# Four 32 KB places as pools in the order of the bytes, behind 72 instead of 64 loads of 8 KB

## The chip, the cores and the metric

The kernel runs on one core of one Trainium2 chip. The metric is the device time of one execution in microseconds. All work is in float32 (some operands of the first half are split into a rounded part and a rest), and all weights come from HBM by DMA.

## The reference, cut to what matters

One encoder layer over 512 tokens of width 1024: a mixer (projections, banded attention, a short convolution, gates), then a layer norm, then a mixture of 16 experts in which each expert picks its 64 best tokens, then a layer norm.

```python
logits = jnp.einsum('bsd,de->bse', x, w_router)
aff = jax.nn.softmax(logits, axis=-1)
top_val, top_idx = lax.top_k(jnp.swapaxes(aff, 1, 2), cap)
xe = x[b_idx, top_idx]
h = jax.nn.silu(jnp.einsum('becd,edf->becf', xe, w_gate)) * jnp.einsum('becd,edf->becf', xe, w_up)
ye = jnp.einsum('becf,efd->becd', h, w_down) * top_val[..., None]
return jnp.zeros_like(x).at[b_idx, top_idx].add(ye)
```

The change touches only how the experts' weights `w_gate`, `w_up` and `w_down` get into the core: 16 experts of 3 matrices of 1024 x 2048, 403 MB in all.

## The kernel before

The mixer runs first, to about 520 us of the span. Then a loop over 8 pairs of experts follows (`for p in range(NPAIR)`). The host lays the weights of a pair out as 12 groups `w_moe[p, g]` of [128 partitions, 4 units, 2048 numbers]. A unit is 8 KB in each of 128 partitions (1 MB in all), a group is 32 KB in each partition (4 MB). So a pair has 48 units: units 0 to 31 are gate and up in turn (four blocks `cb` of eight units, line 963), units 32 to 47 are down (four blocks `cq`, line 1009). A unit of either kind is multiplied once and is then of no more use. Beside these matmuls, TensorE gathers the tokens of the next pair (line 898), turns (lines 913, 984) and scatters the results (line 1022).

`fetch(p, m)` hands out unit m of pair p. Units are numbered through, `n = 48 * p + m`. The first 64 units (`SMALL`) are loads of their own, of 8 KB in a partition, called `w_n`. They go to the places that the list `places` names, in its order:

```python
places = slots[:7] + [(wk, "W2")] + slots[7:8] + [(wk, "W0")] + slots[8:]
places += [(extra, "E")] + slots + [(extra, "E")] + slots[2:] + [(extra, "E")]
```

`slots` are the 20 pools R0 to R19 of 8 KB each, which lie one behind another in a partition. Units 1 to 22 are loaded ahead; from unit 23 on each load takes the place of an older unit. Counted along the list, units 45 to 62 lie on R2 to R19 in this order and unit 63 lies on E. R0 and R1 become the accumulators of the output.

From unit 64 on (pair 1, group 4) the weights come in whole groups `w_p_g` of 32 KB in a partition, into four places of that size. Before, these are one pool with `bufs=4`, opened over the bytes of R4 to R19, which `small.close()` gives back. In the last pair, the groups from 4 on are filled by four loads each.

All these loads are issued by SyncE (SP) on one DMA queue, in the order of the program (`pin`). SP waits, at each load, until the units that lay on the place have been read, and everything behind it in SP's order waits too. `reuse_waits="tile"` makes such a wait one for the tiles that lay on the bytes in question.

Of the kernel before, what the change touches and what calls it, by code (L numbers as in the profile page):

```python
# [10 lines left out]
F32 = mybir.dt.float32  # L11
# [7 lines left out]
P = 128  # L19
# [20 lines left out]
def encoder_layer(ctx: ExitStack, tc: tile.TileContext, x, ln0r, ln0c, w_in, conv_w, sink, w_ao, w_co, w_out,  # L40
# [5 lines left out]
    extra = ctx.enter_context(tc.tile_pool(name="extra", bufs=1))  # L46
# [7 lines left out]
    def shaped(t, shape):  # L54
        names = "abcd"[:len(shape)]
        return t[:, :int(np.prod(shape))].rearrange(f"p ({' '.join(names)}) -> p {' '.join(names)}",
                                                    **dict(zip(names, shape)))
# [279 lines left out]
    src, nm, _ = loads[0]  # L337
# [244 lines left out]

    UNITS, SMALL = 48, 64
    units, groups = {}, {}

    def load_unit(n, pool, tag):
        t = pool.tile([P, 2048], F32, tag=tag, name=f"w_{n}")
        p, m = n // UNITS, n % UNITS  # L590
        pin(nc.sync.dma_start(t, w_moe[p, m // 4][:, m % 4]))
        return t

    def fetch(p, m):

        n = UNITS * p + m
        if n < SMALL:
            if n not in units:
                units[n] = load_unit(n, *places.pop(0))
            return units.pop(n)  # L600
        if not big:
            small.close()
            big.append(ctx.enter_context(tc.tile_pool(name="big", bufs=4, reuse_waits="tile")))
        g, j = m // 4, m % 4
        if j == 0:
            t = big[0].tile([P, 4, 2048], F32, tag="G", name=f"w_{p}_{g}")
            src = w_moe[p, g]
            if p < NPAIR - 1 or g < 4:
                pin(nc.sync.dma_start(t, src))
            for i in range(4 if p == NPAIR - 1 and g >= 4 else 0):  # L610
                if (g, i) != (UNITS // 4 - 1, 3):
                    pin(nc.sync.dma_start(t[:, i], src[:, i]))
                else:
                    ends, begin = shaped(t[:, i], [2, 4, 256]), shaped(src[:, i], [2, 4, 256])
                    for f, n in ((0, 2), (2, 1), (3, 1)):
                        pin(nc.sync.dma_start(ends[:, :, f:f + n, :], begin[:, :, f:f + n, :]))
            groups[p, g] = t
        return groups[p, g][:, j]
# [208 lines left out]
    t = NT - 1  # L827
# [44 lines left out]
    small = ExitStack()  # L872
    accp = ctx.enter_context(tc.tile_pool(name="accp", bufs=1, reuse_waits="tile"))
    slots = [(accp, "R0"), (accp, "R1")]
    for i in range(2, 20):
        slots.append(((ctx if i < 4 else small).enter_context(tc.tile_pool(name=f"r{i}", bufs=1, reuse_waits="tile")), f"R{i}"))
    places = slots[:7] + [(wk, "W2")] + slots[7:8] + [(wk, "W0")] + slots[8:]
    places += [(extra, "E")] + slots + [(extra, "E")] + slots[2:] + [(extra, "E")]
    big = []
    for n in range(1, 23):  # L880
        units[n] = load_unit(n, *places.pop(0))
# [68 lines left out]
    for p in range(NPAIR):  # L950
# [3 lines left out]
        for cb in range(NCB):  # L954
            pss = [mmt(f"p{nm}_{p}_{cb}") for nm in "gu"]
            for kq in range(4):
                for i in range(2):
                    wt = shaped(fetch(p, 8 * cb + 2 * kq + i), [2, 2, 512])
                    for k in range(2):
                        kk = 2 * kq + k  # L960
                        for a in range(2):
                            hs = slice(64 * a, 64 * a + 64)
                            pin(nc.tensor.matmul(pss[i][hs, :], xe[:, kk, hs], wt[:, a, k, :], start=(kk == 0), stop=(kk == KT - 1)))  # L963
                    for _ in range(2 * i if p == cb == 0 else 1 - i):
                        if pend:
                            pend.pop(0)()
# [34 lines left out]
        for cq in range(4):  # L1001
            pd = mmt(f"d_{p}_{cq}")
            for fq in range(4):
                wt = shaped(fetch(p, 32 + 4 * cq + fq), [2, 4, 256])
                for ft in range(4):
                    f = 4 * fq + ft
                    for a in range(2):
                        hs = slice(64 * a, 64 * a + 64)
                        pin(nc.tensor.matmul(pd[hs, :256], hTs[p][:, f, hs], wt[:, a, ft, :], start=(f == 0), stop=(f == 15)))  # L1009
                for _ in range(2):  # L1010
                    if pend:
                        pend.pop(0)()
# [33 lines left out]
    sd, v, r, a2, nb = (q2[:, i, :] for i in range(5))  # L1046
# [80 lines left out]
```

## Time and profile before

| | us |
|---|---|
| median of 3 runs | 1470.6 (1470.47 to 1473.98) |
| profiled execution, its own time | 1468.77 |
| its span, first to last instruction | 1467.0 |
| busy in the span: TensorE matmuls | 1374.0 (94%) |
| busy: VectorE, ScalarE, GpSimd | 396.8, 291.8, 61.8 |

The DMA queue of SP (q1) moves 446.28 of the 451.08 MB. A share of busy time is a mean over stages with different limits: the mixer is a stretch in which the DMA engines are busy some two tenths of the time, the experts one in which they are busy nearly all of it. So the profile is to be read by stretches, and the question at each is which wait ends last there.

### The profile page before, as it was taken

To read this page: it belongs to the slowest core of one execution; us is meant where nothing else is said; L and a number is where in the kernel's file an instruction comes from. 1 tells how busy PE (TensorE), PEld (TensorE's weight loads), DVE (VectorE), ACT (ScalarE), POOL (GpSimd) and SP (SyncE) were. 2 spreads that over 40 slices of the span, in tenths; PEclk is the share of its full clock that TensorE was granted. 3 is DMA by queue.
4 is the path that set the end of the run, shared out by engine and by line. 5 is a ranking of instruction groups with operands and counts; after the bars stand their busy time and mean duration, and the time that the engine had idled before them with its cause. 6 is when DMAs were issued, how large, how long until landed. Compare 5 with 4: busy or idle time off the path is not lost.

```text
span 1467.0 us, 17582 instructions
## 1 busy us (share of the span) xinstructions
PE 1374.0 (94%) x7571; PEld 814.5 (56%) x7571; DVE 396.8 (27%) x892; ACT 291.8 (20%) x580; POOL 61.8 (4%) x46
## 2 busy tenths in 40 slices
PE   7999999999999999998998998899899899899994
PEld 6878778788888843642542452453353264254342
DVE  8567656633335530110010010011011011001015
ACT  5654454422233211000000000000000000000110
POOL 3000000320000005000000000000000000000001
PEclk9999999999999999999999999999999999999998
DMA  4211222322247889968999999999999999999994
GB/s 150 103 67 58 87 86 87 115 101 100 86 144 301 323 299 397 422 265 350 432 430 429 430 432 433 429 429 433 431 430 429 432 431 433 428 432 430 417 422 168
DMA packets 36237, 451.08 MB, mean 307 GB/s; under 512 B 4416, under 2 KB 7104, under 8 KB 9920
## 3 DMA queue, kind: packets, MB, share of 16 engines
q1 hardware_dynamic: 34864, 446.28, 73.4%
q10 hardware_dynamic: 1296, 3.69, 0.8%
q8 instruction: 59, 0.97, 0.3%
q14 instruction: 18, 0.15, 0.0%
HBM read 447.85 MB, written 2.10 MB: 307 GB/s over the span
## 4 chain that ended last, share of the span: by engine, by line
PE 54%; DMA 41%; DVE 3%; ACT 1%; issue 0%; SPq 0%; DVEq 0%
DMA w<-in_w_moe 41%; PE pg L963 6%; PE pu L963 6%; PE d L1009 5%; PE p_x L183 3%; PE p_b L183 3%; PE p_c L183 3%; PE p_q L183 3%; PE p_co L183 3%; PE p_ao L183 3%; PE p_gc L183 3%; PE p_ga L183 3%; PE sc L1022 2%; PE g L898 2%; PE o L524 1%; PE s L484 1%
## 5 line engine op out<-in xcount | busy, mean ns | idle before, releaser
L963 PE MATMUL pg<-w,px 128*64 128x512 f32 x1024 | 248.1, 605 | 50.5 <-DMA w<-in_w_moe 50.4
L1009 PE MATMUL d<-w,hT 128*64 128x256 f32 x2048 | 238.8, 383 | 13.8 <-DMA w<-in_w_moe 13.3
L963 PE MATMUL pu<-w,px 128*64 128x512 f32 x1024 | 245.7, 600 | 0.0
L1009 PEld LDWEIGHTS d<-w,hT 128*64 128x64 f32 x2048 | 143.1, 137 | 101.6 <-issue 30.3
L963 PEld LDWEIGHTS pg<-w,px 128*64 128x64 f32 x1024 | 72.2, 138 | 202.5 <-issue 154.2
L1027 DVE TENSOR_TENSOR acc<-acc,sc 128x256 f32<-128x256 f32 x108 | 45.5, 421 | 335.2 <-PE sc L1022 334.8
L963 PEld LDWEIGHTS pu<-w,px 128*64 128x64 f32 x1024 | 66.0, 136 | 117.9 <-issue 116.1
L972 DVE TENSOR_TENSOR h<-h,pu 128x512 f32<-128x512 f32 x32 | 22.0, 688 | 336.4 <-PE pu L963 336.4
L971 ACT ACTIVATE h<-pg 128x512 f32<-128x512 f32 x32 | 19.1, 597 | 316.2 <-PE pg L963 316.2
L1022 PE MATMUL sc<-ye,px 128*128 128x256 f32 x248 | 74.0, 411 | 0.0
L898 PEld LDWEIGHTS g<-px,xn 128*128 128x128 f32 x512 | 59.0, 192 | 20.5 <-issue 18.7
L1014 ACT COPY ye<-d 128x256 f32<-128x256 f32 x32 | 11.9, 373 | 282.9 <-PE d L1009 282.9
L1022 PEld LDWEIGHTS sc<-ye,px 128*128 128x128 f32 x248 | 40.9, 189 | 44.5 <-issue 42.0
L898 PE MATMUL g<-px,xn 128*128 128x128 f32 x512 | 63.8, 280 | 0.2 <-DVE px L890 0.2
L183 PE MATMUL p_x<-yh,ws_x 128*128 128x512 f32 x128 | 43.9, 398 | 0.0
L183 PE MATMUL p_b<-yh,ws_b 128*128 128x512 f32 x128 | 43.9, 398 | 0.0
L183 PE MATMUL p_c<-yh,ws_c 128*128 128x512 f32 x128 | 43.8, 398 | 0.0
L183 PE MATMUL p_q<-yh,ws_q 128*128 128x512 f32 x128 | 42.1, 395 | 0.0
L496 ACT ACTIVATE pr<-pr,neg 128x256 f32<-128x256 f32 (+1 forms) x64 | 35.2, 553 | 28.7 <-DVE neg L492 28.7
L183 PE MATMUL p_ga<-yh,ws_ga 128*128 128x512 f32 x128 | 40.6, 391 | 0.0
L183 PE MATMUL p_gc<-yh,ws_gc 128*128 128x512 f32 x128 | 40.1, 389 | 0.0
L183 PE MATMUL p_ao<-oh,ws_ao 128*128 128x512 f32 x128 | 40.1, 389 | 0.0
(264 smaller groups left out, 1613.5 us busy)
## 6 DMA issues: line engine op xcount, KB each, us to landing
w<-in_w_moe SPq DMA_DIRECT2D x72, 4096.0 KB, 30.1
w<-in_w_moe SPq DMA_DIRECT2D x95, 1024.0 KB, 12.6
raw_q<-in_w_in SPq DMA_DIRECT2D x4, 1024.0 KB, 4.9
raw_c<-in_w_in SPq DMA_DIRECT2D x4, 1024.0 KB, 4.8
raw_x<-in_w_in SPq DMA_DIRECT2D x4, 1024.0 KB, 4.8
raw_b<-in_w_in SPq DMA_DIRECT2D x4, 1024.0 KB, 4.8
raw_ga<-in_w_in SPq DMA_DIRECT2D x4, 1024.0 KB, 4.8
raw_gc<-in_w_in SPq DMA_DIRECT2D x4, 1024.0 KB, 5.0
```

What stands on the lines that cost most here:

```text
L183: put(nc.tensor.matmul(ps, ws[:, a, k, :], (opnd.lo if b else opnd.hi)(k), start=(k + a + b == 0), stop=ends))
L484: nc.tensor.matmul(ps, q, k[:, g, keys], start=(i == 0), stop=(i == 1))
L496: nc.scalar.activation(p, p, AF.Exp, bias=self.neg[:, i:i + 1], accum_out=self.su[:, i:i + 1])
L524: nc.tensor.matmul(pa[half * 64:half * 64 + 64, :256], vt[g][:, self.b0 + j, :], self.pT[:, j, :, half, :], start=(j == 0), stop=(j == sel ...
L898: pin(nc.tensor.matmul(ps[:, i * P:(i + 1) * P], xt[t][:, (k + i) * P:(k + i + 1) * P], oh1[:, t].rearrange("p a c -> p (a c)"), start=(t ...
L963: pin(nc.tensor.matmul(pss[i][hs, :], xe[:, kk, hs], wt[:, a, k, :], start=(kk == 0), stop=(kk == KT - 1)))
L971: nc.scalar.activation(hb, pss[0], AF.Silu)
L972: nc.vector.tensor_tensor(hb, hb, pss[1], OP.mult)
L1009: pin(nc.tensor.matmul(pd[hs, :256], hTs[p][:, f, hs], wt[:, a, ft, :], start=(f == 0), stop=(f == 15)))
L1014: nc.scalar.copy(ye, pd[:, :256])
L1022: pin(nc.tensor.matmul(ps[:, :256], ohT[:, t * P:(t + 1) * P], ye, start=True, stop=True))
L1027: nc.vector.tensor_tensor(a, a, ps[:, :256], OP.add)
```

## The change

`SMALL` goes from 64 to 72, so that two groups of pair 1 (units 64 to 71) come as eight loads of 8 KB instead of two of 32 KB. They take the places R2 to R9. R2 and R3 now belong to the bytes that are given back as well. The four places of 32 KB are four pools of one buffer each, and group number `n // 4` takes pool `(n // 4) % 4`. Opened one after another over the bytes from R2 on, `big0` lies on R2 to R5, `big1` on R6 to R9, `big2` on R10 to R13 and `big3` on R14 to R17.

```diff
-    UNITS, SMALL = 48, 64
+    UNITS, SMALL = 48, 72
...
         if not big:
             small.close()
-            big.append(ctx.enter_context(tc.tile_pool(name="big", bufs=4, reuse_waits="tile")))
+            big.extend(ctx.enter_context(tc.tile_pool(name=f"big{i}", bufs=1, reuse_waits="tile")) for i in range(4))
         g, j = m // 4, m % 4
         if j == 0:
-            t = big[0].tile([P, 4, 2048], F32, tag="G", name=f"w_{p}_{g}")
+            i = (n // 4) % 4
+            t = big[i].tile([P, 4, 2048], F32, tag=f"G{i}", name=f"w_{p}_{g}")
...
     for i in range(2, 20):
-        slots.append(((ctx if i < 4 else small).enter_context(tc.tile_pool(name=f"r{i}", bufs=1, reuse_waits="tile")), f"R{i}"))
+        slots.append((small.enter_context(tc.tile_pool(name=f"r{i}", bufs=1, reuse_waits="tile")), f"R{i}"))
...
-    places += [(extra, "E")] + slots + [(extra, "E")] + slots[2:] + [(extra, "E")]
+    places += [(extra, "E")] + slots + [(extra, "E")] + slots[2:] + [(extra, "E")] + slots[2:10]
```

The first group is now number 72 / 4 = 18, which takes `big2`. The next ones take `big3`, `big0` and `big1`, and so on round.

On SP the order of the loads at this place was the following before. A name is `w_n` for a unit and `w_p_g` for group g of pair p; the last number is the buffer's. What stands behind "waits" are the counters that SP waits for: PE counts matmuls that have read, and DMAHW0 to DMAHW7 count landings of earlier loads.

```order
L591 DMA w_62_4932<-in_w_moe 128x2048 [waits DMAHW0_49,PE_49]
L591 DMA w_63_4945<-in_w_moe 128x2048 [waits DMAHW1_49,PE_49]
L609 DMA w_1_4_4975<-in_w_moe 128x8192 [waits DMAHW2_49,PE_49]
L609 DMA w_1_5_4999<-in_w_moe 128x8192 [waits DMAHW5_49,DMAHW6_49,DMAHW3_49,DMAHW7_49,DMAHW0_49,PE_49]
L609 DMA w_1_6_5022<-in_w_moe 128x8192 [waits DMAHW4_49]
L609 DMA w_1_7_5046<-in_w_moe 128x8192
L609 DMA w_1_8_5099<-in_w_moe 128x8192 [waits DMAHW2_49,PE_49]
```

The second group load waits for the landings of five earlier loads and for TensorE; the two behind it wait for no matmul any more. With the change the same stretch of SP's order reads:

```order
L591 DMA w_63_4945<-in_w_moe 128x2048 [waits DMAHW1_49,PE_49]
L591 DMA w_64_4956<-in_w_moe 128x2048 [waits DMAHW2_49,PE_49]
L591 DMA w_65_4968<-in_w_moe 128x2048 [waits DMAHW3_49,PE_49]
...
L591 DMA w_70_4998<-in_w_moe 128x2048 [waits DMAHW0_49,PE_49]
L591 DMA w_71_5004<-in_w_moe 128x2048 [waits DMAHW1_49,PE_49]
L610 DMA w_1_6_5045<-in_w_moe 128x8192 [waits DMAHW2_49,PE_49]
L610 DMA w_1_7_5069<-in_w_moe 128x8192 [waits DMAHW3_49,PE_49]
L610 DMA w_1_8_5122<-in_w_moe 128x8192 [waits DMAHW5_49,DMAHW4_49,PE_49]
L610 DMA w_1_9_5159<-in_w_moe 128x8192 [waits DMAHW6_49,DMAHW1_49,DMAHW7_49,DMAHW0_49,PE_49]
```

Eight loads of one unit have moved in where the two group loads `w_1_4` and `w_1_5` stood, each with a wait of its own. The four group loads behind them each wait for TensorE now. On the other engines the order of the instructions is the same as before.

## Rows read from the trace of the kernel before

**Rows 1.** The page's part 2: the span in 40 slices of 36.7 us.

```profile
DMA  4211222322247889968999999999999999999994
GB/s 150 103 67 58 87 86 87 115 101 100 86 144 301 323 299 397 422 265 350 432 430 429 430 432 433 429 429 433 431 430 429 432 431 433 428 432 430 417 422 168
```

**Rows 2.** The chain that ended last: start us, us, what.

```profile
664.24 1.74 PE pg L963 x8
666.84 32.12 DMA w<-in_w_moe
...
1416.53 21.24 DMA w<-in_w_moe
```

**Rows 3.** Four stretches: us, busy (count) by engine, PEclk, DMA share, GB/s.

```profile
600.00:620.00 20.00, 20.00 (x160) 12.42 (x158) 3.37 (x8) 0.74 (x2) 0.00 (x0) 1.00 1.01 421
638.20:640.30 2.10, 2.10 (x15) 1.15 (x12) 0.00 (x0) 0.00 (x0) 0.00 (x0) 1.00 0.00 0
652.50:666.90 14.40, 14.40 (x64) 4.69 (x62) 1.27 (x3) 0.84 (x2) 0.00 (x0) 1.00 0.00 0
...
800.00:900.00 100.00, 91.61 (x564) 44.85 (x560) 10.40 (x24) 6.53 (x14) 0.00 (x0) 1.00 1.00 431
```

**Rows 4.** SP's waits, 600 to 680 us: total us, times, longest.

```profile
SPq L609 <- PE pg L963: 40.2, 2, 25.7
```

**Rows 5.** Five loads, the first at 527.4 us: issue, then us to landing.

```profile
DMA to landing us min/median/max: 4.9/4.9/4.9
...
L591 SPq DMA_DIRECT2D w<-in_w_moe x1: 328/328/328, 624.5 to 624.5; - x1
DMA to landing us min/median/max: 14.1/14.1/14.1
...
L609 SPq DMA_DIRECT2D w<-in_w_moe x1: 332/332/332, 639.4 to 639.4; - x1
DMA to landing us min/median/max: 13.4/13.4/13.4
...
L609 SPq DMA_DIRECT2D w<-in_w_moe x1: 327/327/327, 666.0 to 666.0; - x1
DMA to landing us min/median/max: 13.5/13.5/13.5
...
L609 SPq DMA_DIRECT2D w<-in_w_moe x1: 328/328/328, 676.1 to 676.1; - x1
DMA to landing us min/median/max: 32.6/32.6/32.6
```

**Rows 6.** TensorE in order of time, 628 to 682 us: start, us, instructions.

```profile
628.40 3.67 PE L1009 MATMUL d<-w,hT 128*64 128x256 f32 x32
631.91 1.89 PE L963 MATMUL pg<-w,px 128*64 128x512 f32 x8
...
637.48 1.89 PE L963 MATMUL pg<-w,px 128*64 128x512 f32 x8
...
643.04 1.89 PE L963 MATMUL pg<-w,px 128*64 128x512 f32 x8
...
651.43 1.89 PE L963 MATMUL pg<-w,px 128*64 128x512 f32 x8
...
659.85 1.89 PE L963 MATMUL pg<-w,px 128*64 128x512 f32 x8
...
664.07 1.89 PE L963 MATMUL pg<-w,px 128*64 128x512 f32 x8
...
674.12 1.89 PE L963 MATMUL pu<-w,px 128*64 128x512 f32 x8
679.57 1.94 PE L963 MATMUL pg<-w,px 128*64 128x512 f32 x8 [3.56 <-DMA w<-in_w_moe]
```

**Rows 7.** TensorE's waits for weights, 666 us to the end: total us, times, longest.

```profile
PE pg L963 <- DMA w<-in_w_moe: 50.4, 33, 3.6
PE d L1009 <- DMA w<-in_w_moe: 13.3, 18, 2.6
```

## The prediction, made before the changed kernel ran

> **What bounds the kernel now.** I read the slices of the page first. From slice 20 on (697 us) the DMA engines move some 430 GB/s to the end, and just ahead of that stand two slices with 265 and 350 GB/s [rows 1]. Then the chain that ended last: up to 666 us it is TensorE's own work, and from 666.84 us on it hangs on loads of the experts' weights, 30 us at a time, down to a last piece of 21.24 us that begins at 1416.53 [rows 2]. The stretch view says the same by time: between 800 and 900 us the DMA share is 1.00 at 431 GB/s while TensorE is busy 91.61 of 100 us [rows 3]. So from 667 us to the last landing the time is a sum of bytes at a fixed rate, and an instant in which no packet moved just ahead of that is lost for good, unless TensorE is too slow to use it.
>
> Where did the queue run dry? Two stretches have 0 GB/s: 638.20 to 640.30 and 652.50 to 666.90 [rows 3]. In both, TensorE is busy all the time, so nobody is short of data yet; the price comes later. SP's waits give the cause: two waits of line 609, the loads of 32 KB, for the gate matmuls, 40.2 us together, the longest 25.7 [rows 4].
>
> The timeline of TensorE tells which units these waits are for. Pair 1 begins at 631.91 with unit 48 (gate and up take turns, so gate rows are the even units). The first group load is issued at 639.4, when the gate row of unit 50 (637.48 + 1.89 = 639.37) has ended; the second at 666.0, when that of unit 62 (664.07 + 1.89 = 665.96) has [rows 5, 6]. Units 47 to 50 lie on R4 to R7 and unit 62 lies on R19. So the first group went to the oldest bytes but the second to the last place in the partition, R16 to R19, which was filled last, while R8 to R15 (units 51 to 58) had been read before the gate row of unit 60 at 659.85. SP takes its loads in order, so nothing behind it could start either.
>
> **What the dry queue costs now.** A queued load of 4 MB (4,194,304 bytes) at 431 GB/s takes 9.73 us, one of 1 MB at 421 GB/s takes 2.49 us [rows 3]. Unit 63 landed at 624.5 + 14.1 = 638.6, the first group at 639.4 + 13.4 = 652.8, the second at 666.0 + 13.5 = 679.5 [rows 5]. The steps are 14.2 and 26.7 where 9.73 would do: 4.5 and 17.0 too many, together **21.5 us**. That is more than the 2.1 + 14.4 us without a packet, since a load that finds an empty queue needs 13.4 us from issue to landing instead of 9.73: 3.7 us more.
>
> **The change, part by part.** Bytes, matmuls and the order on every engine but SP stay. Two loads of 4 MB become eight of 1 MB. Up to unit 63 nothing differs.
>
> Eight unit loads. They wait for the units 45 to 52, which lie on R2 to R9. Units 46 and 47 are the down row that ends at 632.1, unit 48 is read at 633.8, unit 50 at 639.4, unit 52 at 644.9 [rows 6]; unit 45 before 628.4. So unit 64 is issued at or before 628.4 and unit 71 at 644.9. If they follow unit 63 without a gap, they land at 638.6 + 2.49 each: unit 64 at 641.1, unit 67 at 648.5, unit 71 at 658.5. Each is thus issued 12.7 to 13.6 us before its landing, about the 14.1 us that unit 63 had in a full queue [rows 5]: there is no gap. Against 4 MB loads they cost 8 x 2.49 - 2 x 9.73 = 0.5 us. TensorE wants unit 64 behind units 62 and 63, not before 664.07 + 2 x 1.89 = 667.9, so it never waits for them; the six more waits on TensorE cost nothing, and its 50.4 + 13.3 us of waits for weights further on are the cover [rows 7].
>
> `w_1_6` on `big2` waits for units 53 to 56. Unit 56 is read at 651.43 + 1.89 = 653.3, 5.2 us before unit 71 lands. That is more than 3.7, so it is queued in time and lands at 658.5 + 9.73 = 668.2. `w_1_7` on `big3` waits for unit 60: 661.7, 6.5 us ahead, landing 678.0.
>
> `w_1_8` on `big0` waits for units 64 to 67, the third block of gate and up. Its first group ends in both kernels at 674.12 + 1.89 = 676.0 [rows 6], because up to there TensorE does not wait. That is 1.9 us before `w_1_7` lands and 1.8 us less than the 3.7 that hide the start. Bounds: it costs nothing if 1.9 us are enough, and 3.7 if the start is not hidden at all. I take the 1.8 between, as the row of 13.4 us to landing gives it: 676.0 + 13.4 or 13.5 = **689.5**.
>
> From there the places come free in time. `w_1_9` waits for unit 71: four units at 1.89 us or less from 676.0, so 683.6 at the latest, 5.9 us ahead of 689.5. After that TensorE needs 0.916 x 9.73 = 8.9 us for a group on the mean [rows 3], less than the 9.73 of the queue. So the lead of SP grows until TensorE waits for weights again, as before.
>
> **The sum.** Before, `w_1_8` landed at 676.1 + 32.6 = 708.7 [rows 5]; now at 689.5. All later loads follow at the same 9.73. Gain: 708.7 - 689.5 = 19.2; by parts 21.5 - 0.5 - 1.8 = **19.2 us**. TensorE can use it, since it gives up 19.2 of the 63.7 us that it waits for weights. What stands behind the last load does not change. The profiled execution took 1468.8 us; 1468.8 - 19.2 = 1449.6. The median of the runs is 1.8 above the profiled time, so I forecast **1451** for the median, a factor of 0.987.
>
> **A row against a rule.** The eight loads rest on 2.49 us for each. The stretch from 600 to 620 us holds nothing but such loads and has 421 GB/s at a DMA share of 1.01 [rows 3], and the queue was full there. A load of 1 MB in an empty queue is another matter: one issued at 527.4, the first after a pause, took 4.9 us to land [rows 5]. The Trainium skill ("DMA: Bandwidth & Descriptors", Anatomy of one DMA) gives a fixed 2.0 us and bytes / 436 GB/s for a DMA on the path through GpSimd; were that paid in turn by each of these loads, it would be 4.4 us for each, 35.2 us for eight, an estimate from that page, and the gain would shrink to some 4 us. The trace does not agree: at 421 GB/s the fixed part is hidden behind the load ahead.
>
> **The rivals.**
> - *Each of the eight loads pays its start* (no change). They land 4.9 us apart, the row of the empty queue: unit 71 at 638.6 + 39.2 = 677.8, `w_1_6` at 687.5, `w_1_7` at 697.2, `w_1_8` at 707.0 instead of 708.7. Gain 1.7 us, median about 1469. For it: the loads come one by one, each with a wait. Against it: issue runs 12.7 us or more ahead. Chance 0.05.
> - *A part is given back in pairs 1 and 2*. All four places are now handed out in step with TensorE, and a group with a gather takes longer than 9.73 us. If the queue ran dry two or three times more at 3.7 us, the gain would be 8 to 12 and the time 1459 to 1463. Against it: the lead of 5.9 us or more after `w_1_8`. Chance 0.06.
> - *Slower: one wait on the youngest units.* If opening the places over R2 to R17 made unit 64 wait, as the second group did, for unit 62 (666.0), the queue would be dry from 638.6, unit 64 would land at 666.0 + 4.9 = 670.9, unit 71 at 688.3, `w_1_7` at 707.8 and `w_1_8` at 717.5, against 708.7: 9 us slower, 1479. The point that decides: the gain is gone when unit 64 lands 19.2 us late, so when it is issued after about 655. For it: the stall of before was of this kind. Against it: the eight loads have a wait each and still take the small pools, whose place the rows show coming free one by one. Chance 0.04.
> - *The change does nothing to the end*, because TensorE is the bound: it would have to need more than it has, but it has 63.7 us of waits to give [rows 7]. I give it no chance of its own.
>
> **How the numbers follow.** The forecast has 0.85, the rivals 0.06, 0.05 and 0.04. The 1451 is that of the likeliest. Its range: a hidden start of `w_1_8` gives 1470.6 - 21.0 = 1449.6, and with a further 1.5 us as the runs scatter 1448; the upper end takes a gain of some 14 us, one more dry start (3.7 us) and the scatter: 1457. That range holds the forecast's 0.85, and the other cases lie above it. A measurement of this kernel tells about 0.3% (4.4 us) from no change. Faster: 0.85 + 0.06 = 0.91; same: 0.05; slower: 0.04.
>
> **What would show it.** Right: no stretch without packets between 620 and 700 us; the loads of units 64 to 71 issued from 628 to 645; `w_1_6` issued at 653, `w_1_7` at 662, `w_1_8` at 676 and landed at 689 or 690; TensorE's first wait for weights not at 676 but in pair 2; its waits down from 63.7 to about 45; last landing and end 19 us earlier, with the stretch behind the last landing unchanged. Wrong: a dry stretch of over 3 us anywhere between 640 and 800, unit loads landing more than 2.6 us apart, or a load rate under 430 GB/s after 700.

## The result, and the profile after

| us | before | after |
|---|---|---|
| median of 4 runs each | 1471.82 (1470.47 to 1473.98) | 1448.88 (1448.42 to 1449.31) |
| profiled execution | 1468.77 | 1448.42 |
| its span | 1467.0 | 1446.7 |

The ratio of the medians is 0.9843 (95%: 0.9826 to 0.986). From profile to profile the gain is 20.3 us. The medians lie 22.9 us apart, since two of the four runs before took 1473 and 1474 us. Below, where the place of a gain matters, profile is compared with profile.

The page's part 2 after, from which the two slices with 265 and 350 GB/s of [rows 1] are gone (slices 18 and 19 now have 420 and 413):

```profile
DMA  4221222322336879999999999999999999999994
GB/s 149 92 83 59 88 88 75 129 87 92 113 117 255 355 288 377 420 420 413 432 429 433 428 434 428 433 431 426 432 431 434 429 428 432 431 430 429 417 422 181
```

The stretches after, the first four the same as in [rows 3]: us, busy (count) by engine, PEclk, DMA share, GB/s.

```profile
600.00:620.00 20.00, 20.00 (x160) 12.41 (x157) 3.37 (x8) 0.75 (x2) 0.00 (x0) 1.00 1.02 422
638.20:640.30 2.10, 2.10 (x15) 1.00 (x12) 0.00 (x0) 0.00 (x0) 0.00 (x0) 1.00 1.02 425
652.50:666.90 14.40, 14.40 (x66) 4.83 (x64) 1.38 (x4) 0.62 (x2) 0.00 (x0) 1.00 1.04 444
...
800.00:900.00 100.00, 93.24 (x572) 45.46 (x570) 10.39 (x24) 7.04 (x15) 0.00 (x0) 1.00 1.00 430
...
660.00:680.00 20.00, 20.00 (x96) 6.83 (x94) 1.11 (x2) 1.69 (x3) 0.00 (x0) 1.00 0.93 386
680.00:700.00 20.00, 20.00 (x106) 8.20 (x103) 1.38 (x2) 2.15 (x4) 0.00 (x0) 1.00 1.01 436
```

Both dry stretches now carry data. One dip is left, a DMA share of 0.93 between 660 and 680 us. It lies from 674.4 to 679.2 us (229 GB/s at a share of 0.67), where `w_1_8` starts.

The loads after, each with its row of issue and the time to landing: units 63 and 71, then `w_1_6`, `w_1_7` and `w_1_8`; they answer to [rows 5].

```profile
L591 SPq DMA_DIRECT2D w<-in_w_moe x1: 328/328/328, 624.7 to 624.7; - x1
...
DMA to landing us min/median/max: 14.5/14.5/14.5
...
L591 SPq DMA_DIRECT2D w<-in_w_moe x1: 328/328/328, 645.2 to 645.2; - x1
...
DMA to landing us min/median/max: 13.9/13.9/13.9
...
L610 SPq DMA_DIRECT2D w<-in_w_moe x1: 328/328/328, 653.6 to 653.6; - x1
...
DMA to landing us min/median/max: 15.2/15.2/15.2
...
L610 SPq DMA_DIRECT2D w<-in_w_moe x1: 328/328/328, 662.0 to 662.0; - x1
...
DMA to landing us min/median/max: 16.5/16.5/16.5
...
L610 SPq DMA_DIRECT2D w<-in_w_moe x1: 328/328/328, 676.3 to 676.3; - x1
...
DMA to landing us min/median/max: 12.4/12.4/12.4
```

The sum of the two numbers is the landing: 639.2, 659.1, 668.8, 678.5 and 688.7. The steps between them are 19.9 for eight units (2.49 each), then 9.7, 9.7 and 10.2.

SP's waits for places of groups after, 600 to 680 us (against the 40.2 us in two waits for gate matmuls of [rows 4]): total us, times, longest.

```profile
SPq L610 <- PE pg L964: 16.0, 2, 8.0
SPq L610 <- PE pu L964: 13.9, 1, 13.9
```

SP still waits: 29.9 us in three waits for a group. All three end while loads are still queued. The first two end 5.5 and 6.8 us before the load ahead has landed, and no time is lost. The last, of 13.9 us for `w_1_8`, ends 2.2 us before that, and here 0.5 us is lost, since the step to its landing is 10.2.

The chain that ended last, after (start us, us, what):

```profile
773.19 23.62 DMA w<-in_w_moe
...
1397.64 19.81 DMA w<-in_w_moe
```

It now hangs on loads from 773.19 us on instead of 666.84 [rows 2]. The last load of the chain lands at 1417.45; before, it landed at 1416.53 + 21.24 = 1437.77. That is 20.3 earlier. Behind it stand 1446.7 - 1417.45 = 29.3 us, and before 1467.0 - 1437.77 = 29.2: that stretch is unchanged. A few loads land later than that one. The last load of all, before and then after, each with its time to landing:

```profile
L616 SPq DMA_DIRECT2D w<-in_w_moe x1: 367/367/367, 1428.9 to 1428.9; - x1
...
DMA to landing us min/median/max: 16.5/16.5/16.5
...
L617 SPq DMA_DIRECT2D w<-in_w_moe x1: 367/367/367, 1410.0 to 1410.0; - x1
...
DMA to landing us min/median/max: 15.0/15.0/15.0
```

It lands at 1445.4 before and 1425.0 after, 20.4 earlier, with 21.6 and 21.7 us behind it.

TensorE's waits for weights after, from 666 us to the end (total us, times, longest), against 50.4 and 13.3 in [rows 7]:

```profile
PE pg L964 <- DMA w<-in_w_moe: 32.9, 23, 3.0
PE d L1010 <- DMA w<-in_w_moe: 10.7, 15, 1.5
```

Together 43.6 instead of 63.7: 20.1 us less. So TensorE, which has the same work to do, gives up nearly the whole gain out of its waits.

### The profile page after: what moved, and what is told of

Read it like the earlier page. It is cut to its first block, busy times and chain, and to the rows that moved or that the text cites. A ratio compares the mean times of both kernels' runs of the same rounds, so it can differ in the third digit from the quotient of the medians.

```text
span 1446.7 us, 17596 instructions
## 1 busy us (share of the span) xinstructions
PE 1373.0 (95%) x7571; PEld 815.2 (56%) x7571; DVE 396.6 (27%) x892; ACT 291.9 (20%) x580; POOL 61.9 (4%) x46
## 4 chain that ended last, share of the span: by engine, by line
PE 60%; DMA 35%; DVE 3%; ACT 1%; issue 0%; SPq 0%; DVEq 0%
DMA w<-in_w_moe 35%; PE pu L964 8%; PE pg L964 8%; PE d L1010 7%; PE p_x L183 3%; PE p_b L183 3%; PE p_c L183 3%; PE p_q L183 3%; PE p_co L183 3%; PE p_ao L183 3%; PE p_gc L183 3%; PE p_ga L183 3%; PE sc L1023 2%; PE g L899 2%; PE o L524 1%; PE s L484 1%
## 6 DMA issues: line engine op xcount, KB each, us to landing
w<-in_w_moe SPq DMA_DIRECT2D x70, 4096.0 KB, 29.3
w<-in_w_moe SPq DMA_DIRECT2D x103, 1024.0 KB, 13.3
```

## The experiments

Theory: the order of the places decides. A group load that waits for units read late stops SP, the queue runs dry, and each microsecond without packets ahead of 700 us is lost at the end. Rivals: it is the eight more unit loads that fill the gap, so that the order matters little; or TensorE's consumption bounds the end after the change. The runs e0, e1, e2 and e4 share a chip with 13 runs of the kernel before (median 1469.63), e5 to e8 another one (1469.02). All diffs are against the changed kernel.

**e1: the order alone.** 64 unit loads as before, R2 and R3 not given back, four pools in the order of the bytes over R4 to R19.

```diff
-    UNITS, SMALL = 48, 72
+    UNITS, SMALL = 48, 64
...
-        slots.append((small.enter_context(tc.tile_pool(name=f"r{i}", bufs=1, reuse_waits="tile")), f"R{i}"))
+        slots.append(((ctx if i < 4 else small).enter_context(tc.tile_pool(name=f"r{i}", bufs=1, reuse_waits="tile")), f"R{i}"))
...
-    places += [(extra, "E")] + slots + [(extra, "E")] + slots[2:] + [(extra, "E")] + slots[2:10]
+    places += [(extra, "E")] + slots + [(extra, "E")] + slots[2:] + [(extra, "E")]
```

> 64 unit loads as before, the four places over R4 to R19 as before, but handed out in the order of the bytes. Theory (a dry queue costs the time, and the order of the places made most of it dry): the first group is issued at 639.4 as before, with some 2 us without a packet and 4.5 us lost; the second waits for unit 54 instead of 62 and is issued at 649, the next two at 657.5 and 666, none late. So 17 of the 20 us come: span 1450, median about 1452.4, some 3.5 us more than with the whole change. Rival (the gain comes from the smaller loads, which free SP from a long wait): no gain, median about 1471.

Measured: 1453.0, ratio 0.9892 (0.9878 to 0.9907). The first two group loads of e1, each issue with its time to landing:

```profile
L610 SPq DMA_DIRECT2D w<-in_w_moe x1: 331/331/331, 639.7 to 639.7; - x1
...
DMA to landing us min/median/max: 13.6/13.6/13.6
...
L610 SPq DMA_DIRECT2D w<-in_w_moe x1: 328/328/328, 649.5 to 649.5; - x1
...
DMA to landing us min/median/max: 13.5/13.5/13.5
```

The second one is issued at 649.5 instead of 666.0 [rows 5] and lands 9.7 behind the first: the long stall is gone. The first one still comes late: unit 63 lands at 640.2, the first group at 653.3, a step of 13.1 where 9.73 would do.

**e2: the eight loads alone.** 72 unit loads from R2 on, but one pool of four buffers as before.

```diff
-            big.extend(ctx.enter_context(tc.tile_pool(name=f"big{i}", bufs=1, reuse_waits="tile")) for i in range(4))
+            big.append(ctx.enter_context(tc.tile_pool(name="big", bufs=4, reuse_waits="tile")))
...
-            t = big[i].tile([P, 4, 2048], F32, tag=f"G{i}", name=f"w_{p}_{g}")
+            t = big[0].tile([P, 4, 2048], F32, tag="G", name=f"w_{p}_{g}")
```

> 72 unit loads, but the four places are one pool of four buffers as before, now over R2 to R17. The first group then lies on R2 to R5, where the youngest units 64 to 67 are. Theory: the queue is dry from the landing of unit 71 (659) until unit 67 has been read (676) and the first group lands at 690 instead of 669, 21 us late: median about 1470, no gain against before. Rival (the smaller loads are the gain): median about 1449.

Measured: 1468.05, ratio 0.9991 (0.9982 to 1.0001). A stretch of e2 and its first group load (the columns as above):

```profile
658.60:677.60 19.00, 19.00 (x89) 6.52 (x90) 1.53 (x3) 1.69 (x3) 0.00 (x0) 1.00 0.00 1
```

```profile
L610 SPq DMA_DIRECT2D w<-in_w_moe x1: 328/328/328, 676.7 to 676.7; - x1
```

Unit 71 lands at 658.9, and then next to nothing flows until the first group is issued at 676.7, when units 64 to 67 have been read. The stall has only moved: the eight loads keep the queue filled up to 658.9, and then the pool hands out first the bytes on which units 64 to 67 lie, which are read only at 676. So the eight loads by themselves gain next to nothing in this layout. Eight loads ahead of a pool that starts at other bytes were not run.

**e4: the order, begun at R2, without the eight loads.** 64 unit loads; R2 and R3 are given back, so the four pools lie on R2 to R17 and the first group (number 16) takes `big0` on R2 to R5.

```diff
-    UNITS, SMALL = 48, 72
+    UNITS, SMALL = 48, 64
...
-    places += [(extra, "E")] + slots + [(extra, "E")] + slots[2:] + [(extra, "E")] + slots[2:10]
+    places += [(extra, "E")] + slots + [(extra, "E")] + slots[2:] + [(extra, "E")]
```

> 64 unit loads as before, four pools in the order of the bytes over R2 to R17, so that the first group takes the oldest bytes of all (units 45 to 48). Theory: the first group is issued when unit 48 has been read, 634, which is 5 us before unit 63 lands; the next at 645, 653 and 662, each 3.7 us or more ahead. No dry stretch, and eight unit loads less at 0.06 us: the same time as with the whole change, 1448 to 1449.5. Rival (the eight more unit loads are needed to carry the queue over): 3 us or more above it.

Measured: 1450.66, ratio 0.9871 (0.9856 to 0.9887). The first group is issued at 638.3, ahead of unit 63's landing at 628.9 + 14.4 = 643.3. From unit 63's issue to the last landing e4 takes 800.4 us, the changed kernel 800.3. Thus e4 gives the whole gain, and the eight more loads add none to it: what they would do is done by the two oldest units, on R2 and R3. The median is 1.2 us above the expected range, since two of the four runs took 1452.7 and 1452.8. In the profiled one of these the first expert matmul stands at 529.8 us, 4.2 later than in the first profile of the changed kernel.

**e0: the changed kernel again**, on the chip of e1, e2 and e4.

> The changed kernel once more, on the chip of these experiments: 1448 to 1450 for comparison.

Measured: 1450.3, ratio 0.9874 (0.9854 to 0.9895), so 19.3 us less than 1469.63. The profiled execution of e0 took 1455.3 us; its first expert matmul stands at 531.25 us instead of 525.61, so those microseconds lie in the mixer, which the change does not touch. From unit 63's issue to the last landing it takes 801.6 us, against 800.3 in the first profile. That measure leaves the mixer out, and I use it below: before it is 1445.4 - 624.5 = 820.9, and 804.4 in e1. So of the 20.6 us that the change gains by it, the order over R4 to R19 (e1) gives 16.5, and beginning the round at R2 (e4) another 4.0.

**e5, e6, e7: the round shifted.** e4 with the place of a group shifted by one, two or three; 2 and 3 stand in the line for e6 and e7.

```diff
-            i = (n // 4) % 4
+            i = (n // 4 + 1) % 4
```

> The kernel with 64 unit loads and four places over R2 to R17, with the round of places begun one place later: the first group waits for unit 52 instead of 48. Theory (the queue's dry time is paid one for one): it is issued at 645 when unit 63 has landed at 639; it lands 12.4 to 13.4 us after its issue, at 658, where 649 would do. No wait after that. 8 to 9 us above the round that begins at the oldest bytes: 1458 to 1460. Rival (TensorE takes up a dry queue of a few us, since it reads unit 64 only at 668): no change, 1450.

> The same, begun two places later: the first group waits for unit 56, is issued at 653.5 and lands at 666 or 667, just before TensorE wants it at 668. Theory: 17 us above the round that begins at the oldest bytes, 1466 to 1468, though TensorE waits for nothing there. Rival: no change, since the data come in time.

> The same, begun three places later: the first group waits for unit 60, is issued at 662 and lands at 674.5 to 675.5, which is the stall of the kernel before in one piece and longer. Theory: 25 to 26 us above the round that begins at the oldest bytes, 1475, slower than before by 0.3%. Rival (only what TensorE waits at 668 is paid): 6 us, 1457.

| | first group issued | its landing | unit 63's issue to last landing | median | ratio (95%) |
|---|---|---|---|---|---|
| e4 | 638.3 | 653.1 | 800.4 | 1450.66 | 0.9871 (0.9856 to 0.9887) |
| e5 | 645.1 | 657.5 | 809.4 | 1458.63 | 0.9936 (0.992 to 0.9953) |
| e6 | 653.6 | 665.8 | 817.6 | 1466.09 | 0.9981 (0.9971 to 0.9991) |
| e7 | 661.8 | 674.3 | 826.3 | 1474.67 | 1.0046 (1.003 to 1.0062) |

Unit 63 was issued at 628.9 in e4 and at 624.5 to 624.8 in the others, so the first two columns of e4 are some 4 us late. Counted from unit 63's issue, the first group lands 24.2, 32.8, 41.0 and 49.8 us later, in steps of 8.6, 8.2 and 8.8, and the end comes 9.0, 8.2 and 8.7 later: paid one to one. In e6 TensorE hardly waits at first. A stretch of e6 and, from its timeline, two gate rows behind that (start, us, and in brackets the idle time ahead with what ended it):

```profile
638.50:654.00 15.50, 15.50 (x78) 6.19 (x74) 1.80 (x3) 1.55 (x3) 0.00 (x0) 1.00 0.01 3
```

```profile
668.48 1.89 PE L964 MATMUL pg<-w,px 128*64 128x512 f32 x8
...
676.75 1.94 PE L964 MATMUL pg<-w,px 128*64 128x512 f32 x8 [0.50 <-DMA w<-in_w_moe]
```

Next to nothing moves for 15.5 us, from the last packets of unit 63 to the first ones of the group (the few GB/s are other loads), and TensorE does not miss it: its first wait, 22 us later, is 0.50 us. Still the end comes 17.2 us later than in e4, and 17.3 later than in the changed kernel. Its waits for weights, 640 us to the end:

```profile
PE pg L964 <- DMA w<-in_w_moe: 46.4, 32, 3.0
PE d L1010 <- DMA w<-in_w_moe: 13.3, 18, 2.2
```

They add up to 59.7 us, 16.1 more than in the changed kernel (and 11.7 more than the 48.0 of e4, whose TensorE was busy 4.8 us less from unit 63's issue on). That is the clearest view of how a dry queue is paid: not where it is dry, but in TensorE's later waits, when the weights that were loaded ahead have been used up.

In e7 it does wait, for 6.03 us as soon as it comes to the first group. The row of e7's timeline, and two stretches of it:

```profile
674.45 3.68 PE L964 MATMUL pg<-w,px 128*64 128x512 f32 x8 [6.03 <-DMA w<-in_w_moe]
```

```profile
668.00:674.00 6.00, 0.41 (x2) 0.00 (x0) 0.69 (x1) 0.00 (x0) 0.00 (x0) 0.84 1.01 437
674.00:679.00 5.00, 4.55 (x12) 1.57 (x12) 0.00 (x0) 0.00 (x0) 0.00 (x0) 0.51 0.97 419
```

This run has the same loads, bytes and matmuls as e4, and is slower than the kernel before. The order of the places alone spans 24 us.

**e8: less work for TensorE.** The changed kernel without the scatter of pairs 1 to 6: its matmuls and the sums behind them are left out.

```diff
                 def go():
+                    if 0 < p < NPAIR - 1:
+                        return
```

> The changed kernel without the scatter matmuls and their sums in pairs 1 to 6 (the output lacks those experts), some 12 us of TensorE's time in each of six pairs. Theory (after the change the queue of the weights still sets the end): the same time within 2 us, 1448 to 1451, with TensorE's waits for weights longer by some 70 us. Rival (TensorE has become the bound or shares it): 10 to 70 us faster.

Measured: 1449.54, ratio 0.9874 (0.9858 to 0.9891). Part 1 of e8's page and its waits for weights, 666 us to the end:

```profile
PE 1330.7 (92%) x7379; PEld 809.2 (56%) x7379; DVE 356.1 (25%) x796; ACT 291.9 (20%) x580; POOL 61.8 (4%) x46
```

```profile
PE pg L964 <- DMA w<-in_w_moe: 59.6, 32, 3.8
PE d L1010 <- DMA w<-in_w_moe: 29.8, 21, 2.9
```

TensorE's busy time falls from 1373.0 to 1330.7 and its waits rise from 43.6 to 89.4 us. The time stays. So the queue is still the bound after the change, and a faster TensorE gains nothing: from unit 63's issue to the last landing e8 takes 800.2 us, the changed kernel 800.3. My expectation of the waits was too high, 45.8 us more instead of some 70. They answer to 42.3 us less work, where six times 12 us were expected. The mean granted clock is 0.977 instead of 0.991 and the gate matmuls take 620 ns on the mean instead of 607, 6.4 us in all, so that part of what was left out is spent again in slower matmuls.

## Why the prediction was right, step by step

- *The dry queue costs 21.5 us at the end.* Right, and tested three ways: e1 takes the long stall away and gains 16.5 of the 820.9 us, e2 keeps a stall of the same kind and gains 1.1, and e5 to e7 put one back in steps, paid for one to one.
- *The cause is the order of the places, by which the second group waits for unit 62.* Shown by e1 against e2: the order without the eight loads gains, the eight loads without the order do not. e5 to e7 show it once more, with the order as the only thing that differs.
- *Eight unit loads cost 0.5 us.* The step from unit 63 to unit 71 is 19.9 us against 2 x 9.73 = 19.5: 0.4. They land 2.49 apart, as forecast, each issued some 14 us ahead. The rival in which each pays its start is refuted. But the working never asked whether they were needed: e4 shows that they are not, once the round begins at R2. The estimate of 4.4 us each takes the fixed part of the Trainium skill ("DMA: Bandwidth & Descriptors", Anatomy of one DMA) as paid in turn by each load. The 2.49 us of this trace do not bear that out.
- *The landings*, forecast and measured: unit 71 658.5 and 659.1, `w_1_6` 668.2 and 668.8, `w_1_7` 678.0 and 678.5. The 0.5 or 0.6 throughout is unit 63, which landed 0.6 later than before.
- *The start of `w_1_8` costs 1.8 us.* Mis-sized. It was issued at 676.3, 2.2 ahead of `w_1_7`'s landing, and landed 12.4 later instead of 13.4: a step of 10.2, so 0.5 us lost. The form of the term holds: the working took a lead of 13.4 - 9.73 = 3.7 us to hide the start, and with 12.4 it is 2.7, of which a lead of 2.2 leaves 0.5. e4 agrees: there the same load, with a lead of 1.9, landed 12.3 after its issue, a step of 10.4. Before the change `w_1_8` landed at 708.7, now at 688.7: 20.0 instead of 19.2, by 1.3 us less lost at its start and the 0.6 of unit 63 taken off. That is the whole difference between forecast and profile, but for 0.3 us that the later loads saved.
- *From `w_1_9` on the lead grows until TensorE waits again, first in pair 2.* Right. From 680 to 700 us the share is 1.01. Before, TensorE waited 3.56 us for the gate row at 679.57 us [rows 6]. Its timeline after, around 676 us, and its first wait for weights behind that:

```profile
674.34 1.89 PE L964 MATMUL pu<-w,px 128*64 128x512 f32 x8
676.06 1.89 PE L964 MATMUL pg<-w,px 128*64 128x512 f32 x8
...
796.85 1.94 PE L964 MATMUL pg<-w,px 128*64 128x512 f32 x8 [1.63 <-DMA w<-in_w_moe]
```

  The rival in which part of the gain is given back in pairs 1 and 2 did not come: the steps to the last landing are the same, 736.7 us from `w_1_8` before and 736.3 after.
- *The slower rival, a wait on the youngest units*, did not come here, but a wait on late units can be slower than before: e7, whose first group waits for units 57 to 60, ends 0.46% above the kernel before. The prediction put the point at which the gain is gone at an issue of about 655, for a first load of one unit. With a first load of a whole group, e6, issued at 653.6, still has 0.19% of gain, and e7, at 661.8, has none; the point itself was not run.
- *TensorE's waits down to about 45.* 43.6. *The rest behind the last landing unchanged.* 21.6 and 21.7 behind the last landing of all, 29.2 and 29.3 behind the last load of the chain.
- *A load rate under 430 GB/s after 700 us as a sign of being wrong* was drawn too tight. Single slices behind that lie a little under it after (426 and 417, for example) as they did before (429 and 417), while 700 to 800 us has 431 and 800 to 900 us 430. It tells nothing against the mechanism.
- *The median.* 1451 forecast; 1448.88 and, in the second set, 1450.3 measured. The factor was forecast as 0.987; it is 0.9843 in the first set, in which two of the four runs before were long, and 0.9874 in the second. The 1.8 that I added to the profiled time for the scatter of the runs depends on which runs are drawn: between two executions of the changed kernel the first expert matmul differs by 5.6 us. Whether the long runs before have the same cause was not traced.

What stays open: whether any order or lead would give back the last 0.5 us of `w_1_8`, which is below what the medians of the runs can tell; why a group lands 12.4 us after its issue here and 13.4 before; and why the mixer's time varies.

## What to carry to other kernels

Where one in-order queue feeds a kernel that is bound by bytes, read for each load which reader frees its place, and hand the places out in the order in which they are read. In such a kernel a stall of the queue is paid at the end even if no engine waits when it happens, so look for stretches with 0 GB/s and not for engines that idle. Judge a wait at the issuer by its lead and not by its length; the lead is the time from the issue that ends the wait to the landing of the load ahead. For loads of 4 MB, a lead of 3.7 us lost nothing here (e0), one of 2.2 us lost 0.5 (the changed kernel), and one of 0.5 us lost 3.4 (e1).

## What the runs showed of the hardware that was not expected

Into a dry queue a load of 4 MB took 12.2 to 12.5 us from issue to landing in e2 and e5 to e7. With a short lead over the landing ahead it took no longer: 12.4 with 2.2 us in the changed kernel, 12.3 with 1.9 in e4. Only what is left of the start is then lost: with the lead of 2.2 us (`w_1_8`) the step was 10.2 instead of 9.7, and with 3.7 us in e0 (issued at 681.9, landed 13.4 later) it was 9.7, no loss. In the kernel before and in e1 the time into a dry or nearly dry queue was 13.4 to 13.6. These two are the runs whose four places lie on R4 to R19, while in all the others they lie on R2 to R17; whether that makes the difference of 1 us was not tested.

After TensorE's longest wait in e7, 6.03 us, the next stretch of 5 us had a granted clock of 0.51, the level of 1.2 GHz: eight matmuls that take 1.89 us took 3.68 there.
